# A third seven-product pair in each gate and up group, and low parts by an adding DMA, in a float32 encoder layer

## The chip, the cores and the metric

The kernel runs on one core of a Trainium2 chip. The metric is the device time of one execution in microseconds (us). TensorE is called PE here, VectorE DVE, ScalarE ACT, GpSimd POOL and SyncE SP, as in the profile.

## The reference

One layer of an encoder on 256 tokens of width 2048, all in float32: four mixers side by side, cross attention over 256 memory rows, and a gated feed-forward network, each behind an RMS norm and with a residual; then a last norm. The change is in the feed-forward part:

```python
D_FF = ((8 * D_MODEL // 3 + 255) // 256) * 256        # 5632
def swiglu(h, w_gate_up, w_down):
    gate, up = jnp.split(h @ w_gate_up, 2, axis=-1)
    return (jax.nn.silu(gate) * up) @ w_down
...
    x = x + swiglu(rms_norm(x, norm_g[l, 2]), w_gate_up[l], w_down[l])
return rms_norm(x, final_norm_g)
```

## The kernel before

**Float32 from three matmuls.** A weight W is split into a rounded high part `wh` (ACT copies it to the type that PE multiplies in one pass) and a low part `wl` = W - `wh` (DVE subtracts). Activations are split in the same way. A product is then hi x wh + hi x wl + lo x wh: `part` (L412) issues these three matmuls, 128 x 128 by 128 x 512 each, and all of PE's work in the stage goes through it (L414 to L416).

**The weight stream.** All weights lie in device memory in the order of use, in slabs of 128 x 2048 (1 MB, 16 blocks of 128 columns). `Stream` loads one slab at a time into one of three `raw` buffers (SP issues, L97), and makes halves of 1024 columns: `_half` (L102) with ACT's copy at L124 and DVE's subtraction at L125, into buffers from a pool of three and one extra. `_fill` keeps the half in use and three more made. A raw buffer is free again when the last half of its slab is split.

**Seven products for eight.** A slab of kind N gives four (column block, k) pairs, each with two row halves of the 256 tokens: 4 x 2 x 3 = 24 matmuls. A slab of kind S holds a 2 x 2 arrangement of tiles (two k, two column blocks) and is multiplied by a scheme of seven products instead of eight, 7 x 3 = 21 matmuls. Its sums of weights are made on the fly by `_sums` (L130): four phases (of 1024, 512, 1024 and 1024 columns), four additions on DVE at L137, and a cast (L140) and a subtraction (L141) for each phase. The sums of activations, `z`, are made once by `combine`.

**The gate and up stage.** `gate_up` computes 11 groups of 512 gate and 512 up columns. The first is plain (`gemm_rows`), the other ten go through `paired_rows` with the plan `GROUP` of eight slabs. In a group the gate's two row halves end in PSUM banks `a0` and `a1`, the up's in `b0` and `b1`, and four more banks hold the products `1`, `5`, `6`, `7` that several results share. When the group's last S is done, `mixed` combines these four (ACT's copy at L1034 is its first step), and `gated` adds `a0` and `a1` (L264, `g<-g,pg`) and applies silu (L1044). At the end of the group `upped` adds `b0` and `b1`, multiplies, transposes and stores the result to device memory (`store_turned`, L525). `fetch` brings stored tiles back (L530) and splits them into the `f` tiles of the down product. The next group takes the banks of `a0` and `a1` with its first matmuls.

**Order.** The code issues splits, products and background work (`Background`: `fetch`, `combine` and the like, polled between products) in one program order; a scheduler then fixes the order on each engine before the run. Engines work through their queues in that order, and so does SP with its loads and POOL with its transfers.

**The down stage** (`down`) has 44 k tiles, the `f` list: eight `act` tiles, the `f` tiles, then the tiles that share memory with `z`, then those that share it with `h3`, the input of the gate and up stage. The last two kinds can only be filled when the gate and up stage is over (the second `fetch` of `gate_up`).

Of the kernel before, what the change touches and what calls it, by code (L numbers as in the profile page):

```python
# [13 lines left out]
F32 = mybir.dt.float32  # L14
F32R = mybir.dt.float32r
# [4 lines left out]
ALU = mybir.AluOpType  # L20
# [3 lines left out]
P = 128  # L24
R = 256
D = 2048
KT = D // P
DFF = 5632
FT = DFF // P
# [12 lines left out]
LATE = 12  # L42

GATE_UP = 1920 // 16 + 8
GROUP = "NNSNNSNN"

DOWN = GATE_UP + 80
PASSES = "NNNNNNSNNSNNSNNSNNSNNN", "NNSNSNSNSNSNSNNNNNNNNN"

PAIRED = {a + i for a, plan in [(GATE_UP + 8 * j, GROUP) for j in range(10)] + [(DOWN, PASSES[0]), (DOWN + 22, PASSES[1])]  # L50
          for i, x in enumerate(plan) if x == "S"}

LAG, OWED, SOON, FAR = 1.3, 0.9, 0.01, 18.0
V_NG = 0
# [16 lines left out]
class Stream:  # L71


    def __init__(self, tc, pools, W, bg):
        self.tc, self.nc, self.W, self.bg = tc, tc.nc, W, bg
        self.rawp, self.wp = pools
        self.order = []
        self.n = self.made = 0
        self.after = []
        self.halves = []  # L80
        self.at = self.phase = 0
        self.raw = None
        self.extra = None
        self.places = []

    def _buffers(self, n, m):

        pool = self.extra if self.extra and len(self.halves) % 4 == 3 else self.wp
        at = 48 if any(a <= n < b for a, b in ROWS) else 8
        return (pool.tile([P, 1088], F32R, name=t, tag=t)[:, at:at + m] for t in ("wh", "wl"))  # L90

    def _load(self, n):

        nc = self.nc
        self.raw = self.rawp.tile([P, 2048], F32, name="raw", tag="raw")
        for a, b in zip(CUTS[n], CUTS[n][1:]) if n in CUTS else [(0, 1024), (1024, 2048)] if self.after else [(0, 2048)]:
            (nc.scalar if (n, a) == (0, 0) else nc.sync).dma_start(self.raw[:, a:b], self.W[n // 16][:, a:b])  # L97
            if self.after:
                self.after.pop(0)()

    def _half(self):

        nc, n = self.nc, self.made
        if n % 16 == 0 and self.phase == 0:
            self._load(n)
        if n // 16 in PAIRED:
            return self._sums()
        self.made += 8
        o = (n % 16) * P
        r = self.raw[:, o:o + 1024]  # L110
        if n >= NBLK - HELD:
            parts = []
            for a in (0, 512):
                wh, wl = self.places.pop(0)
                nc.scalar.copy(wh, r[:, a:a + 512])
                nc.vector.tensor_tensor(out=wl, in0=r[:, a:a + 512], in1=wh.bitcast(F32), op=ALU.subtract)
                parts.append((wh, wl))
            self.bg.dve(1024)
            self.halves.append(parts)
            return  # L120
        wh, wl = self._buffers(n, 1024)
        edges = [0, 256, 512, 1024] if n == 0 else [0, 512, 1024] if n == 8 else [0, 1024]
        for a, b in zip(edges, edges[1:]):
            nc.scalar.copy(wh[:, a:b], r[:, a:b])  # L124
            nc.vector.tensor_tensor(out=wl[:, a:b], in0=r[:, a:b], in1=wh[:, a:b].bitcast(F32), op=ALU.subtract)  # L125
        self.bg.dve(1024)
        self.halves.append((wh, wl))
# [108 lines left out]
class Block:  # L236
# [758 lines left out]
    def mlp(self):  # L995
        tc, nc, act = self.tc, self.nc, self.act
        with tc.tile_pool(name="fp", bufs=1) as fp:
            self.gap(fp, 192)
            f = [fp.tile([P, 512], F32R, name=f"f{i}") for i in range(16)]
            z = [fp.tile([P, 1024], F32R, name=f"z{i}") for i in range(2)]  # L1000
            f = act[4:12] + f + [z[i // 2][:, i % 2 * 512:i % 2 * 512 + 512] for i in range(4)] + self.h3
            with tc.tile_pool(name="wy", bufs=1) as self.st.extra:
                self.gap(self.st.extra, 64)
                with tc.tile_pool(name="gp", bufs=2) as gp:
                    self.gate_up(gp, f, z)
# [7 lines left out]
    def gate_up(self, gp, f, z):  # L1013

        nc = self.nc
        box, g, stored = {}, {}, []

        def gate(ps):
            for r in range(2):
                g[r] = gp.tile([P, 512], F32, name=f"g{r}", tag=f"g{r}")  # L1020
                nc.scalar.activation(g[r], ps[r], AF.Silu, scale=box["col"][:, r:r + 1])

        def up(j, ps, h=None):
            h = h or [gp.tile([P, 512], F32, name="h", tag="h") for _ in range(2)]
            for r in range(2):
                u = gp.tile([P, 512], F32, name="u", tag="u")
                self.stt(h[r], ps[r], box["col"][:, r:r + 1], g[r], ALU.mult, ALU.mult)
                self.store_turned(self.ff, 4 * j, r, u, h[r])
            stored.append(self.bg.now)

        def mixed(q1, q5, q6, q7):

            g[0], g[1], h[0], h[1] = (gp.tile([P, 512], F32, name=n, tag=n) for n in ("g0", "g1", "h", "h"))
            nc.scalar.copy(g[0], q1)  # L1034
            self.tt(h[0], g[0], q6, ALU.add)
            self.tt(g[1], h[0], q7, ALU.add)
            self.tt(h[0], q5, h[0], ALU.subtract)
            self.tt(h[1], q5, g[1], ALU.subtract)

        def gated(*ps):  # L1040

            for r in range(2):
                self.tt(g[r], g[r], ps[r], ALU.add)
                nc.scalar.activation(g[r], g[r], AF.Silu, scale=box["col"][:, r:r + 1])  # L1044

        def upped(j, ps):

            for r in range(2):
                self.tt(h[r], h[r], ps[r], ALU.add)
            up(j, h, h)  # L1050

        h = {}

        def fetch(k0, k1, ahead, pause, wait=0):

            m = {}
            for k in range(k0, k1 + ahead):
                if k < k1:
# [22 lines left out]
        arrival = lambda: gp.tile([P, R], F32, name="ar", tag="ar", bufs=4)  # L1081
        last = self.bg.add(self.arrive(self.xf[1], 3, arrival, self.put3, FAR), go=True)
        col = self.bg.add(norm())
        ps = self.gemm_rows("w_gate_up", [0, DFF], self.h3,
                            parts=[(range(8), [0]), (range(8, 12), [0]), (range(12), [1]), (range(12, 16), [0]), (range(12, 16), [1])],
                            before=lambda n: n in (1, 3) and self.bg.drain(self.late if n == 1 else last))
        self.bg.drain(col)
        def combined():
            for ks, z in sums:
                yield from self.combine(z, *(self.h3[k] for k in ks))  # L1090
                yield
        sums = [((2 * i, 2 * i + 1), z[i]) for i in range(GROUP.count("S"))]
        comb = self.bg.add(combined())
        gate(ps[0])
        up(0, ps[1])
        early = self.bg.add(fetch(0, FT - 20, 3, 2.0, 15))
        self.bg.drain(comb)
        for j in range(1, DFF // 512):
            upped(j, self.paired_rows("w_gate_up", [j * 512, DFF + j * 512], self.h3, sums, GROUP, mixed, gated)[0])
        self.bg.drain(early)  # L1100
        self.fetch = self.bg.add(fetch(FT - 20, FT, 6, SOON))

    def down(self, f, sp):

# [751 lines left out]
```

## Time and profile before

| | |
|---|---|
| Time, median of 3 runs | 1443.23 us (1443.13 to 1443.74) |
| The profiled execution: time, span | 1444.41 us, 1442.6 us |
| Granted PE clock | 0.999 |
| Device memory read, written | 298.52 MB, 20.45 MB |
| Raw slab loads of 1024 KB | 246 |

Times in rows are microseconds from the start of the span, durations microseconds unless marked ns. In a timeline row "x3" merges three instructions that follow each other, and what stands in brackets is the idle time ahead of the row and who ended it. In a row of the windows stand, after the window and its length, the busy time and the count of PE, of PE's weight loads, DVE, ACT and POOL, then the granted clock, the DMA engines' mean busy share and GB/s. A row by form has the busy sum, the mean in ns of one, and the idle time ahead with its releasers.

### The profile page before, as it was taken

Reading aid. Unit: us, or ns where it says so; the run is one execution under the profiler, and the core shown is the slowest. Engines: PE = TensorE matmul, PEld = TensorE weight load, DVE = VectorE, ACT = ScalarE, POOL = GpSimd, SP = SyncE. Lnnn points to the kernel's source line nnn. Section 1 sums busy time; section 2 is a strip of 40 time slices with the busy share of each in tenths; the row PEclk is TensorE's granted clock in tenths of the full one; section 3 lists DMA queues with packets and bytes.
Section 4 is the critical chain, followed back from the end, with each engine's and each line's share of the span. In section 5 each row is a group of like instructions: output and inputs, shape, how many; then the busy total and the mean of one; then the engine's idle time right before and its main releaser. Section 6 shows DMA issues by size and latency. Waiting matters only on the chain.

```text
span 1442.6 us, 18337 instructions
## 1 busy us (share of the span) xinstructions
PE 1431.6 (99%) x6631; PEld 1189.5 (82%) x6631; DVE 1121.8 (78%) x1673; ACT 793.9 (55%) x1138; POOL 207.1 (14%) x276
## 2 busy tenths in 40 slices
PE   9999999999999999999999999999999999999997
PEld 7888888888888888888888888888888888788886
DVE  6667868777877667676676888888888888978984
ACT  6566565446655555555554555545555555545553
POOL 0000100013212233530421001111100002000000
PEclk9999999999999999999999999999999999999999
DMA  9886554556667788964785666566566557545553
GB/s 352 288 290 248 204 207 159 176 173 219 202 198 233 235 263 265 274 204 155 238 257 188 233 233 230 198 242 232 200 235 237 211 182 266 204 188 185 223 215 136
DMA packets 60076, 320.19 MB, mean 222 GB/s; under 512 B 9517, under 2 KB 11214, under 8 KB 28368
## 3 DMA queue, kind: packets, MB, share of 16 engines
q1 hardware_dynamic: 46208, 281.11, 54.8%
q0 software_dynamic: 13344, 37.24, 9.6%
q8 instruction: 52, 0.85, 0.2%
q10 hardware_dynamic: 432, 0.66, 0.1%
q14 instruction: 40, 0.33, 0.1%
HBM read 298.52 MB, written 20.45 MB: 221 GB/s over the span
## 4 chain that ended last, share of the span: by engine, by line
PE 98%; DVE 1%; DMA 0%; ACT 0%; issue 0%; SPq 0%; DVEq 0%
PE pg L414 27%; PE pg L416 27%; PE pg L415 27%; PE pg L362 4%; PE pg L363 2%; PE pm L415 2%; PE pm L416 2%; PE pm L414 2%; PE pm L1309 1%; PE pm L988 1%; PE pm L959 1%; DMA raw<-in_W 0%; PE pm L1718 0%; PE pm L960 0%; PE pm L1483 0%
## 5 line engine op out<-in xcount | busy, mean ns | idle before, releaser
L125 DVE TENSOR_TENSOR wl<-raw,wh 128x1024 fp32r<-128x1024 f32 (+1 forms) x441 | 528.0, 1213 | 182.8 <-ACT wh L124 179.4
L124 ACT CAST wh<-raw 128x1024 fp32r<-128x1024 f32 (+1 forms) x441 | 455.3, 1043 | 318.0 <-PE pg L416 252.6
L414 PE MATMUL pg<-wh,act 128*128 128x512 f32 (+1 forms) x1514 | 591.4, 391 | 0.8 <-ACT wh L124 0.8
L415 PE MATMUL pg<-wl,act 128*128 128x512 f32 (+1 forms) x1514 | 589.7, 390 | 1.3 <-DVE wl L125 1.1
L416 PE MATMUL pg<-wh,act 128*128 128x512 f32 (+1 forms) x1514 | 589.5, 389 | 0.0
L414 PEld LDWEIGHTS pg<-wh,act 128*128 128x128 f32 x1514 | 284.6, 188 | 61.2 <-issue 1.5
L415 PEld LDWEIGHTS pg<-wl,act 128*128 128x128 f32 x1514 | 284.5, 188 | 60.7 <-DVE wl L125 2.1
L416 PEld LDWEIGHTS pg<-wh,act 128*128 128x128 f32 x1514 | 284.4, 188 | 59.4 <-DVE act L264 0.2
L140 ACT CAST wh<-raw 128x1024 fp32r<-128x1024 f32 x124 | 116.8, 942 | 194.6 <-PE pg L416 111.9
L141 DVE TENSOR_TENSOR wl<-raw,wh 128x1024 fp32r<-128x1024 f32 x124 | 134.7, 1089 | 65.9 <-ACT wh L140 65.9
L362 PE MATMUL pg<-act,wh 128*128 128x512 f32 x256 | 90.5, 395 | 0.0
L137 DVE TENSOR_TENSOR raw<-raw 128x512 f32<-128x512 f32 x124 | 85.6, 690 | 2.9
L363 PE MATMUL pg<-act,wl 128*128 128x256 f32 x256 | 71.8, 281 | 0.0
L525 POOL DMA_DIRECT2D hidden<-u x22 | 16.6, 760 | 372.3 <-DVE u L523 372.3
L362 PEld LDWEIGHTS pg<-act,wh 128*128 128x128 f32 x256 | 48.1, 188 | 10.4
L363 PEld LDWEIGHTS pg<-act,wl 128*128 128x128 f32 x256 | 48.2, 188 | 0.2
L530 POOL DMA_DIRECT2D tmp<-hidden x44 | 38.8, 887 | 62.4 <-DMA hidden<-u 34.0
L416 PE MATMUL pg<-wh,f 128*128 128x512 f32 x110 | 42.8, 389 | 0.0
L415 PE MATMUL pg<-wl,f 128*128 128x512 f32 x110 | 42.8, 389 | 0.0
L414 PE MATMUL pg<-wh,f 128*128 128x512 f32 x110 | 42.8, 389 | 0.0
L525 POOL DMA_DIRECT2D features<-tmp x32 | 22.7, 715 | 95.7 <-DVE tmp L523 95.7
L530 POOL DMA_DIRECT2D ar<-features x24 | 21.1, 886 | 24.8 <-ACT wh L124 12.4
(358 smaller groups left out, 1469.5 us busy)
## 6 DMA issues: line engine op xcount, KB each, us to landing
raw<-in_W SPq DMA_DIRECT2D x246, 1024.0 KB, 5.0
raw<-in_W SPq DMA_DIRECT2D x11, 512.0 KB, 7.2
hidden<-u POOLq DMA_DIRECT2D x22, 256.0 KB, 3.8
tmp<-hidden POOLq DMA_DIRECT2D x44, 128.0 KB, 3.3
features<-tmp POOLq DMA_DIRECT2D x32, 128.0 KB, 2.7
ar<-features POOLq DMA_DIRECT2D x24, 128.0 KB, 6.2
k<-in_mem SPq DMA_DIRECT2D x8, 256.0 KB, 6.7
keys<-k POOLq DMA_DIRECT2D x8, 256.0 KB, 7.5
```

Of the source, the lines that this page charges most:

```text
L124: nc.scalar.copy(wh[:, a:b], r[:, a:b])
L125: nc.vector.tensor_tensor(out=wl[:, a:b], in0=r[:, a:b], in1=wh[:, a:b].bitcast(F32), op=ALU.subtract)
L137: nc.vector.tensor_tensor(out=s[out], in0=s[a], in1=s[b], op=ALU.add)
L140: nc.scalar.copy(wh, src)
L141: nc.vector.tensor_tensor(out=wl, in0=src, in1=wh.bitcast(F32), op=ALU.subtract)
L362: self.nc.tensor.matmul(p[:, :], wh, slot[:, :], start=start, stop=False)
L363: self.nc.tensor.matmul(p[:, 0:R], wl, slot[:, 0:R], start=False, stop=stop)
L414: self.nc.tensor.matmul(p, hi, wh, start=start, stop=False)
L415: self.nc.tensor.matmul(p, hi, wl, start=False, stop=False)
L416: self.nc.tensor.matmul(p, lo, wh, start=False, stop=stop)
L525: self.nc.gpsimd.dma_start(to[r], u.rearrange("p (k c) -> p k c", c=P))
L530: self.nc.gpsimd.dma_start(t.rearrange("p (g t) -> p g t", t=32), src)
```

## The change

- `GROUP` becomes `NNSNSNSN`: a third S instead of an N. `z` gets a third buffer, `f` gives up two tiles, so 22 instead of 20 of the 44 down tiles are filled after the gate and up stage.
- In the N slabs at places 0, 1, 3 and 5 of a group the second half is made by `_begin`, one slab ahead: ACT copies it to `wh` (rounded), ACT writes the negated rounded weights to `wl`, and a DMA from POOL adds the weights from device memory to `wl`. DVE has no part in it. The two buffers for it are a pool of their own, `lows`. The slab is loaded to its `raw` buffer at that time, one slab earlier in program order than before.
- To make room, `g0` and `g1` have one buffer instead of two, the transposed result goes into `g` instead of a tile `u`, and the last arriving tiles use the space of `h`.
- `combine` runs as background work of the first group instead of behind it, with a pause of 3.0 before each pair.

```diff
-GROUP = "NNSNNSNN"
+GROUP = "NNSNSNSN"
...
+LOW = "LL.L.L.."
+LOWS = {GATE_UP + 8 * j + i for j in range(10) for i, x in enumerate(LOW) if x == "L"}
...
+    def _begin(self, n):
+        nc = self.nc
+        if n not in self.raws:
+            self._load(16 * n)
+        wh, wl = (self.lows.tile([P, 1024], F32R, name=t, tag=t) for t in ("wh", "wl"))
+        src = self.raws[n][:, 1024:2048]
+        nc.scalar.copy(wh, src)
+        nc.scalar.mul(wl, src, -1.0)
+        nc.gpsimd.dma_start(wl, self.W[n][:, 1024:2048], accum_op=ALU.add)
+        self.early[n] = wh, wl
+
     def _half(self):
+        n = self.made // 16
+        begin = self.lows and self.made % 16 == 0 and self.phase == 0 and n + 1 in LOWS
+        self._entry()
+        if begin:
+            self._begin(n + 1)
+
+    def _entry(self):
         nc, n = self.nc, self.made
         if n % 16 == 0 and self.phase == 0:
-            self._load(n)
+            if n // 16 not in self.raws:
+                self._load(n)
+            self.raw = self.raws.pop(n // 16)
         if n // 16 in PAIRED:
             return self._sums()
         self.made += 8
+        if n % 16 and n // 16 in self.early:
+            self.halves.append(self.early.pop(n // 16))
+            return
...
-            f = [fp.tile([P, 512], F32R, name=f"f{i}") for i in range(16)]
-            z = [fp.tile([P, 1024], F32R, name=f"z{i}") for i in range(2)]
+            f = [fp.tile([P, 512], F32R, name=f"f{i}") for i in range(14)]
+            z = [fp.tile([P, 1024], F32R, name=f"z{i}") for i in range(3)]
...
-                u = gp.tile([P, 512], F32, name="u", tag="u")
                 self.stt(h[r], ps[r], box["col"][:, r:r + 1], g[r], ALU.mult, ALU.mult)
-                self.store_turned(self.ff, 4 * j, r, u, h[r])
+                self.store_turned(self.ff, 4 * j, r, g[r], h[r])
...
-        early = self.bg.add(fetch(0, FT - 20, 3, 2.0, 15))
+        early = self.bg.add(fetch(0, FT - 22, 3, 2.0, 15))
         self.bg.drain(comb)
-        for j in range(1, DFF // 512):
-            upped(j, self.paired_rows("w_gate_up", [j * 512, DFF + j * 512], self.h3, sums, GROUP, mixed, gated)[0])
+        with lp as self.st.lows:
+            self.gap(self.st.lows, 96)
+            for j in range(1, DFF // 512):
+                upped(j, self.paired_rows("w_gate_up", [j * 512, DFF + j * 512], self.h3, sums, GROUP, mixed, gated)[0])
+            self.st.lows = None
         self.bg.drain(early)
-        self.fetch = self.bg.add(fetch(FT - 20, FT, 6, SOON))
+        self.fetch = self.bg.add(fetch(FT - 22, FT, 6, SOON))
```

More of the change, by code (lines that the diff above doesn't have):

```diff
@@ L82, in __init__ @@
         self.raw = None
-        self.extra = None
+        self.extra = self.lows = None
         self.places = []
+        self.raws, self.early = {}, {}
     def _buffers(self, n, m):
@@ L94, in _load @@
         nc = self.nc
-        self.raw = self.rawp.tile([P, 2048], F32, name="raw", tag="raw")
+        raw = self.raws[n // 16] = self.rawp.tile([P, 2048], F32, name="raw", tag="raw")
         for a, b in zip(CUTS[n], CUTS[n][1:]) if n in CUTS else [(0, 1024), (1024, 2048)] if self.after else [(0, 2048)]:
-            (nc.scalar if (n, a) == (0, 0) else nc.sync).dma_start(self.raw[:, a:b], self.W[n // 16][:, a:b])
+            (nc.scalar if (n, a) == (0, 0) else nc.sync).dma_start(raw[:, a:b], self.W[n // 16][:, a:b])
             if self.after:
                 self.after.pop(0)()
-    def _half(self):
+    def _begin(self, n):
[8 more added lines that the diff above has]
+        self.early[n] = wh, wl
+    def _half(self):
+        n = self.made // 16
[4 more added lines that the diff above has]
+    def _entry(self):
         nc, n = self.nc, self.made
         if n % 16 == 0 and self.phase == 0:
-            self._load(n)
+            if n // 16 not in self.raws:
+                self._load(n)
+            self.raw = self.raws.pop(n // 16)
         if n // 16 in PAIRED:
@@ L998, in mlp @@
             self.gap(fp, 192)
-            f = [fp.tile([P, 512], F32R, name=f"f{i}") for i in range(16)]
-            z = [fp.tile([P, 1024], F32R, name=f"z{i}") for i in range(2)]
-            f = act[4:12] + f + [z[i // 2][:, i % 2 * 512:i % 2 * 512 + 512] for i in range(4)] + self.h3
+            f = [fp.tile([P, 512], F32R, name=f"f{i}") for i in range(14)]
+            z = [fp.tile([P, 1024], F32R, name=f"z{i}") for i in range(3)]
+            f = act[4:12] + f + [z[i // 2][:, i % 2 * 512:i % 2 * 512 + 512] for i in range(6)] + self.h3
             with tc.tile_pool(name="wy", bufs=1) as self.st.extra:
                 self.gap(self.st.extra, 64)
-                with tc.tile_pool(name="gp", bufs=2) as gp:
-                    self.gate_up(gp, f, z)
+                with tc.tile_pool(name="gp", bufs=1) as gp:
+                    self.gate_up(gp, f, z, tc.tile_pool(name="lp", bufs=2))
                 with tc.tile_pool(name="sp", bufs=1) as sp:
@@ L1011, in mlp, with gate_up @@
                 self.down_end(f, *end)
-    def gate_up(self, gp, f, z):
+    def gate_up(self, gp, f, z, lp):
         nc = self.nc
@@ L1023, in up @@
         def up(j, ps, h=None):
-            h = h or [gp.tile([P, 512], F32, name="h", tag="h") for _ in range(2)]
+            h = h or [gp.tile([P, 512], F32, name="h", tag="h", bufs=2) for _ in range(2)]
             for r in range(2):
-                u = gp.tile([P, 512], F32, name="u", tag="u")
                 self.stt(h[r], ps[r], box["col"][:, r:r + 1], g[r], ALU.mult, ALU.mult)
-                self.store_turned(self.ff, 4 * j, r, u, h[r])
+                self.store_turned(self.ff, 4 * j, r, g[r], h[r])
             stored.append(self.bg.now)
         def mixed(q1, q5, q6, q7):
-            g[0], g[1], h[0], h[1] = (gp.tile([P, 512], F32, name=n, tag=n) for n in ("g0", "g1", "h", "h"))
+            g[0], g[1], h[0], h[1] = (gp.tile([P, 512], F32, name=n, tag=n, bufs=b) for n, b in (("g0", 1), ("g1", 1), ("h", 2), ("h", 2)))
             nc.scalar.copy(g[0], q1)
@@ L1079, in norm, with combined @@
             yield
-        arrival = lambda: gp.tile([P, R], F32, name="ar", tag="ar", bufs=4)
+        spare = [gp.tile([P, 512], F32, name="h", tag="h", bufs=2) for _ in range(2)]
+        spare = iter([x[:, i:i + R] for x in spare for i in (0, R)])
+        arrival = lambda: next(spare)
         last = self.bg.add(self.arrive(self.xf[1], 3, arrival, self.put3, FAR), go=True)
         col = self.bg.add(norm())
+        def combined():
+            for ks, z in sums:
+                yield 3.0
+                yield from self.combine(z, *(self.h3[k] for k in ks))
+        sums = [((2 * i, 2 * i + 1), z[i]) for i in range(GROUP.count("S"))]
+        comb = self.bg.add(combined())
         ps = self.gemm_rows("w_gate_up", [0, DFF], self.h3,
@@ L1087, in gate_up @@
         self.bg.drain(col)
[L1088 to L1093, printed above, removed]
         gate(ps[0])
         up(0, ps[1])
-        early = self.bg.add(fetch(0, FT - 20, 3, 2.0, 15))
+        early = self.bg.add(fetch(0, FT - 22, 3, 2.0, 15))
         self.bg.drain(comb)
-        for j in range(1, DFF // 512):
-            upped(j, self.paired_rows("w_gate_up", [j * 512, DFF + j * 512], self.h3, sums, GROUP, mixed, gated)[0])
+        with lp as self.st.lows:
[3 more added lines that the diff above has]
+            self.st.lows = None
         self.bg.drain(early)
-        self.fetch = self.bg.add(fetch(FT - 20, FT, 6, SOON))
+        self.fetch = self.bg.add(fetch(FT - 22, FT, 6, SOON))
     def down(self, f, sp):
```

## The prediction

> **What bounds the kernel now.** I read the page's busy table and chain first, then the stage of the change product by product, then the queues inside one product.
>
> ```profile
> PE 1431.6 (99%) x6631; PEld 1189.5 (82%) x6631; DVE 1121.8 (78%) x1673; ACT 793.9 (55%) x1138; POOL 207.1 (14%) x276
> PE 98%; DVE 1%; DMA 0%; ACT 0%; issue 0%; SPq 0%; DVEq 0%
> ```
>
> TensorE (PE) is busy for 99% of the span and makes up 98% of the chain that ended last. A saved matmul can therefore be a saved pitch of PE, provided the others keep up. The line that copies `q1` in `mixed` runs once per gate and up group, so it is the clock of the stage. The windows cut the stage at that line.
>
> ```profile
> L1034 ACT COPY g<-pm x10: 579/579/580, 806.7 to 1186.1; 128x512 f32<-128x512 f32 x10
> ```
>
> ```profile
> 806.71:848.87 42.16, 42.16 (x188) 34.93 (x187) 36.27 (x44) 22.93 (x29) 5.03 (x6) 1.00 0.63 225
> 1059.65:1101.80 42.15, 42.15 (x188) 34.92 (x187) 36.01 (x44) 21.69 (x25) 5.04 (x6) 1.00 0.62 225
> ```
>
> Nine periods take 379.4 us, 42.16 each. By the plan a group has 2 S slabs of 7 products x 3 matmuls and 6 N slabs of 24, so 186 matmuls: 42.16 / 186 = 0.2267 us a matmul. (The windows count 188, because the modelled ends overlap the cut.) PE is busy for the whole of each window, so no group loses anything now. One S slab lasts 21 x 0.2267 = 4.76 us, one N slab 5.44, one N half 2.72.
>
> **Matmuls removed.** A third S in place of an N takes out 3 of 186 matmuls: 0.68 us a group, 10 groups, **6.80 us**. That is all that the change can gain. The other parts decide how much of it stays.
>
> **VectorE (DVE), the amount.** Rows of the stage by form, and one run of splits:
>
> ```profile
> L137 DVE TENSOR_TENSOR raw<-raw 128x512 f32<-128x512 f32 x80 | 55.2, 690 | 1.9
> L141 DVE TENSOR_TENSOR wl<-raw,wh 128x512 fp32r<-128x512 f32 x20 | 13.7, 686 | 0.0
> ```
>
> ```profile
> 1084.88 0.61 DVE L264 TENSOR_TENSOR tmp<-tmp 128x128 f32<-128x128 f32 x2
> 1086.29 1.23 DVE L141 TENSOR_TENSOR wl<-raw,wh 128x1024 fp32r<-128x1024 f32 x1 [0.79 <-ACT wh L140]
> 1087.64 4.63 DVE L125 TENSOR_TENSOR wl<-raw,wh 128x1024 fp32r<-128x1024 f32 x4
> ```
>
> A split in a run costs 4.63 / 4 = 1.16 us. An S slab costs four additions at 0.69, three full splits and a half one at 0.69: 6.93. It replaces an N slab's two splits (2.32), and four low parts leave DVE (4.64). The difference is 6.93 - 2.32 - 4.64 = -0.03 us a group: DVE still works 36 us, now in 41.48 instead of 42.16, 87% against 85%. By amount it is no bound. Between two S slabs there is now one N slab instead of two, but its second half is a low one: 6.93 + 1.16 = 8.1 us of DVE in 4.76 + 5.44 = 10.2 us of PE. That fits as well.
>
> **DVE, the order at the end of a group.** The third S stands at place 6 of 8, the second stood at place 5. So `mixed` and `gated` have one N slab (5.44 us) before the next group needs the banks of `a0` and `a1`, where they had two (10.88). PE, then DVE, after an S slab at place 5:
>
> ```profile
> 1058.44 0.39 PE L414 MATMUL pm<-wh,act 128*128 128x512 f32 x1
> ```
>
> ```profile
> 1059.77 1.23 DVE L141 TENSOR_TENSOR wl<-raw,wh 128x1024 fp32r<-128x1024 f32 x1 [0.69 <-ACT wh L140]
> 1061.19 3.50 DVE L125 TENSOR_TENSOR wl<-raw,wh 128x1024 fp32r<-128x1024 f32 x3 [0.20 <-ACT wh L124]
> 1064.61 0.68 DVE L264 TENSOR_TENSOR h<-g,pm 128x512 f32<-128x512 f32 x1
> 1065.21 1.22 DVE L125 TENSOR_TENSOR wl<-raw,wh 128x1024 fp32r<-128x1024 f32 x1
> 1066.34 0.68 DVE L264 TENSOR_TENSOR g<-h,pm 128x512 f32<-128x512 f32 x1
> 1066.94 0.68 DVE L264 TENSOR_TENSOR g<-g,pg 128x512 f32<-128x512 f32 x1
> 1067.54 0.68 DVE L264 TENSOR_TENSOR h<-pm,h 128x512 f32<-128x512 f32 x1
> 1068.14 0.68 DVE L264 TENSOR_TENSOR h<-pm,g 128x512 f32<-128x512 f32 x1
> 1068.74 1.21 DVE L125 TENSOR_TENSOR wl<-raw,wh 128x1024 fp32r<-128x1024 f32 x1
> 1069.87 0.68 DVE L264 TENSOR_TENSOR g<-g,pg 128x512 f32<-128x512 f32 x1
> 1070.47 1.22 DVE L125 TENSOR_TENSOR wl<-raw,wh 128x1024 fp32r<-128x1024 f32 x1
> 1073.83 1.27 DVE L264 TENSOR_TENSOR h<-h,pg 128x512 f32<-128x512 f32 x2
> 1075.02 1.41 DVE L268 SCALAR_TENSOR_TENSOR h<-h,rc,g 128x512 f32<-128x512 f32 x2
> 1076.35 1.30 DVE L523 STREAM_TRANSPOSE u<-h 128x512 f32<-128x512 f32 x2
> ```
>
> The S slab starts at 1058.44. The two `g<-g,pg` rows are what frees the banks: `a0` at 1067.62 (+9.18), `a1` at 1070.55 (+12.11). Before, the next group wanted them at 4.76 + 10.88 = +15.64 and, its second row half three matmuls later, +16.32. Afterwards it wants them at +10.20 and +10.88. With today's order and pace `a0` has 1.0 us left and `a1` is 1.2 us late. Two things pull it in. Five splits stand ahead of the second `g<-g,pg`; with the new plan one of the next five halves is a low one, so one split (1.16) falls away. And a low half holds none of the four split buffers, so the last splits of the S slab, which today wait for PE to give one back, may start up to half an N half earlier. What is left is between 0 and 1.2 us a group; I take 0.05, so **+0.5 us** over ten groups, with 0 and 12 as the ends. `upped` (about 3.7 us, from 1073.83) then starts behind it and ends some 15 us after the S began, long before the first S of the next group at place 2 wants DVE.
>
> **The adding DMA.** No row shows an addition in a transfer. What can be read is how long it may take. The tightest is slab 5. Its raw load reuses the buffer of slab 2, an S, whose last split ends some 2.56 us after it began (1059.77 + 1.23 - 1058.44 in the S above). Then the load, two ACT passes, the issue:
>
> ```profile
> raw<-in_W SPq DMA_DIRECT2D x246, 1024.0 KB, 5.0
> ...
> hidden<-u POOLq DMA_DIRECT2D x22, 256.0 KB, 3.8
> ```
>
> ```profile
> L124 ACT CAST wh<-raw 128x1024 fp32r<-128x1024 f32 x118 | 121.4, 1050 | 53.8 <-PE pg L416 47.9 <-PE pm L416 5.9
> ...
> L530 POOL DMA_DIRECT2D tmp<-hidden x32 | 28.2, 888 | 38.9 <-DMA hidden<-u 34.0 <-ACT wh L140 4.9
> ```
>
> 2.56 + 5.0 + 2 x 1.05 + 0.89 = 10.6 us; PE wants the low part at 4.76 + 5.44 + 4.76 + 2.72 + 0.23 = 17.9. So 7.3 us are allowed; for slab 1 the same sum over S, N, N and an N half gives 8.0, slabs 0 and 3 have no less. The 512 KB are bounded below by 3.8 (256 KB, plain) and above by 10 (twice the 5.0 of 1024 KB). I take 6, between the rows and nearest to the 1024 KB one with some sharing, so **0 us**; at the upper end 2.7 us are missed in slab 5, 2.0 in slab 1. The cover is the low pool's second buffer and the start one slab ahead. GpSimd (POOL) issues in order: four times 0.89 is added to its 5.0 us a group, but the L530 row sat 34.0 us behind landings of `hidden<-u`, and an adding DMA queued there waits too.
>
> ```profile
> 1083.79 3.52 POOL L530 DMA_DIRECT2D tmp<-hidden x4 [4.93 <-ACT wh L140]
> ```
>
> With a group's start at 1058.44 + 15.64 = 1074.08 these stand 9.7 to 13.2 us into it, in places 1 and 2, ahead of slab 3's adding DMA, which is wanted only about 10 us later.
>
> Load: queue by queue in one group,
>
> ```profile
> q1 hardware_dynamic: 1152, 8.39, 53.3%
> q0 software_dynamic: 352, 1.05, 8.8%
> ```
>
> four halves add 2.1 MB: at q1's rate 13%, at q0's 18%, so the DMA share goes from 0.62 to about 0.78. The Trainium skill (Collectives: The Full Stack, the section on the bandwidth ceiling and why AG, RS and AR differ) says that a reduction in the DMA engines is slow because each add reads two sources, and measures it at half the rate of a copy. By that rule the 13% become 27% and the share 0.89, an estimate; no run here shows it yet, and the sum above does not use it.
>
> **ScalarE (ACT).** 3.6 casts for the S, less 2, plus 4 negations at 1.05: about 6 us more on 22 of 41.48. It is idle enough. What matters is that a copy waiting for a raw load holds the queue: between 0 and the 2 us of one such stall. The order on a queue goes by what is ready rather than by the program: the `q1` copy runs ahead of three casts that the code issues before it,
>
> ```profile
> 1059.64 0.58 ACT L1034 COPY g<-pm 128x512 f32<-128x512 f32 x1
> 1060.11 2.98 ACT L124 CAST wh<-raw 128x1024 fp32r<-128x1024 f32 x3
> ```
>
> so I take 0.
>
> **The passage into `down`.** Two more of the 44 `f` tiles are filled late (22 instead of 20), where DVE is already the chain:
>
> ```profile
> 1223.94 1.35 issue
> ...
> 1238.79 1.15 DVE wl L125
> ...
> 1239.98 0.50 PE pg L415
> ```
>
> ```profile
> PE pg L415 <- DVE wl L125: 0.6, 1, 0.6
> PE pg L415 <- DVE wl L141: 0.2, 1, 0.2
> ```
>
> PE loses 0.8 us here today. Two splits of a 256-wide tile at half the 0.69 row add 0.7, and `upped` of the last group ends up to 1.3 us later against PE. So 0 to 2.0 more; I take **+1.0**. The combinations moved into the first product have a cover: DVE is idle for over half of it.
>
> ```profile
> 765.00:775.00 10.00, 10.00 (x46) 8.29 (x45) 4.02 (x5) 5.10 (x6) 0.00 (x0) 1.00 0.60 210
> ```
>
> Single `g` and the transpose into `g` cost nothing: the store lands in 3.8 us, the next write to `g` comes some 25 us after it.
>
> **Sum.** -6.80 + 0.5 + 0 + 1.0 = -5.3 us against the profiled execution's 1444.41 (span 1442.6): 1439.1. The median of the three runs, 1443.23, is 1.2 below that execution, so **1438.0**. About 0.2% (2.9 us) is what a measurement can tell from no change.
>
> **Rivals.**
> *The banks come late.* DVE's order at the end of a group stays as it is, or an ACT negation slips in ahead of the casts, and `a1` is late by 1.2 to 2 us each time: +12 to +20, so -6.8 + 1 + 12 = about 1449, and up to 1457. It decides from 0.6 us a group on. For it: the static order above; against it: the split that falls away. Chance 0.17, a third of it with so little delay that the result is within 0.2%.
> *The adding DMA lands late.* From 7.3 us on, each microsecond costs 10 us for slab 5, from 8.0 on another 10 for slab 1. At 10 us: 27 + 20, less the gain, about 1484; at 8 us, 1445. For it: no row shows such a transfer, and the rule of two reads (Trainium skill, above) points to the 1024 KB row or worse. Chance 0.16.
> *The stage was not PE's after all*, the slots are filled by waits, and nothing changes: against it stand the full PE windows. Chance 0.05.
> Forecast, 1436.4 (nothing lost) to 1440.3: 0.62.
>
> **Range and chances.** 1436.3 to 1449: that leaves out the upper end of both slow rivals, about 0.17, and very little below. Faster 0.62, same 0.11 (a third of the banks' case, and the last rival), slower 0.27. The forecast's own range is 1436.4 to 1440.3.
>
> **What would show it.** Right: the period of the `q1` copy at 41.48, PE full in each window, DVE near 36 us a group, landing of the adding DMA under 7 us. Wrong: PE waiting for a `g<-g,pg` at a group's first matmul (banks), for a low tile from a DMA at the second half of slabs 5 or 1 (late landing), or over 2.8 us of PE waits between the last group and the first S of `down`.

## The result: slower, by what fills the low halves

The changed kernel takes 1464.22 us (median of 4 runs, 1461.92 to 1466.33) against 1443.49 for the kernel before in the same runs: a ratio of 1.0141, interval 1.0128 to 1.0154. The forecast was 1438.0 with a range up to 1449.0; size and sign are wrong. The profiled execution took 1463.94 us, its span is 1461.8. Line numbers below are those of each kernel's own code; in the kernel after, the matmuls are L443 to L445, a plain half's cast and split L153 and L154, those of a sum L169 and L170, the low half's copy, negation and adding DMA L112 to L114, the bank additions L293 and the `q1` copy L1062.

The busy table and the chain that ended last, of after:

```profile
PE 1437.1 (98%) x6601; PEld 1184.4 (81%) x6601; DVE 1125.1 (77%) x1703; ACT 839.7 (57%) x1198; POOL 242.4 (17%) x314
PE 19%; DVE 2%; DMA 1%; ACT 0%; issue 0%; ACTq 0%; DVEq 0%
```

The chain could be followed back to about 1130 us only and says nothing of most groups. PE runs 30 matmuls fewer and yet is busy for 5.5 us more, at a granted clock of 0.995 instead of 0.999: a first sign that some of them ran more slowly. The windows over nine periods of the `q1` copy (window and length, then busy time and count of PE, weight loads, DVE, ACT and POOL, granted clock, DMA share, GB/s), before and then after:

```profile
806.70:1186.10 379.40, 379.40 (x1676) 314.33 (x1675) 323.41 (x387) 202.32 (x231) 38.26 (x46) 1.00 0.62 222
```

```profile
817.70:1207.70 390.00, 379.25 (x1630) 305.45 (x1628) 320.16 (x400) 238.17 (x279) 69.42 (x80) 0.99 0.86 261
```

A period is 43.33 us (390.0 / 9) instead of 42.16, where 41.48 was forecast. PE was full before and now is idle for 10.75 us. DVE's work hardly changed. ACT's rose by 35.9 us, the DMA share from 0.62 to 0.86. PE's waits of after, from 760 to 1300 us:

```profile
PE pg L444 <- DVE wl L154: 5.3, 5, 2.2
PE pm L443 <- ACT wh L169: 2.9, 2, 2.5
PE pg L444 <- DMA wl<-in_W: 2.4, 4, 1.0
PE pm L444 <- DVE wl L170: 2.0, 3, 0.8
PE pg L443 <- DVE g L293: 0.5, 2, 0.3
PE pg L443 <- ACT wh L153: 0.3, 1, 0.3
```

Three kinds stand here: ordinary splits that come late (L153, L154, L169, L170), the adding DMA, and the bank additions. (The longest wait of the first row, 2.2 us, stands in the passage into `down`, in the later tables too.) The view leaves out short idles and the slow matmuls behind a stall. So I also added up, between 760 and 1290 us, by how much each matmul's start lay beyond 0.2267 us after the one before, and put each piece down to the last wait named ahead of it. After loses 26.3 us: late splits 14.6, the adding DMA 4.3, banks 3.0, the passage into `down` 4.4. Before loses 1.6, all in the passage. 26.3 - 1.6 - 6.8 saved = 17.9 of the 19.2 us between the spans. The figures below called "lost" are from this sum.

**How an ordinary split comes late.** The timelines of ACT, DVE and PE of after, at one place:

```profile
900.21 1.05 ACT L112 CAST wh<-raw 128x1024 fp32r<-128x1024 f32 x1 [1.57 <-DMA raw<-in_W]
901.16 1.05 ACT L113 ACTIVATE wl<-raw 128x1024 fp32r<-128x1024 f32 x1
902.12 2.92 ACT L153 CAST wh<-raw 128x1024 fp32r<-128x1024 f32 x3
```

```profile
903.18 3.50 DVE L154 TENSOR_TENSOR wl<-raw,wh 128x1024 fp32r<-128x1024 f32 x3 [3.10 <-ACT wh L153]
```

```profile
904.47 0.50 PE L444 MATMUL pg<-wl,act 128*128 128x512 f32 x1 [0.76 <-DVE wl L154]
```

ACT first waits for a raw load, then makes the two passes for the next slab's low half, and only then the cast of a half that is wanted at once. DVE sat idle for 3.10 us until this cast, PE until DVE's split. The two passes take 1.91 us of ACT's queue and PE waited for 0.76: without them the cast would have been in time, by about 1 us. Without the hold of 1.57 us ahead of them it would have been, too. ACT is busy for only 61% of the nine periods, but its order is fixed.

The dearest case is the hold in front of slab 5's passes:

```profile
976.41 1.05 ACT L112 CAST wh<-raw 128x1024 fp32r<-128x1024 f32 x1 [6.02 <-DMA raw<-in_W]
977.36 1.05 ACT L113 ACTIVATE wl<-raw 128x1024 fp32r<-128x1024 f32 x1
978.32 1.98 ACT L169 CAST wh<-raw 128x1024 fp32r<-128x1024 f32 x2
```

```profile
979.40 0.80 PE L443 MATMUL pm<-wh,z 128*128 128x512 f32 x1 [2.49 <-ACT wh L169]
980.66 0.80 PE L444 MATMUL pm<-wl,z 128*128 128x512 f32 x1 [0.47 <-DVE wl L170]
981.25 0.63 PE L445 MATMUL pm<-wh,z 128*128 128x512 f32 x1
981.68 0.63 PE L443 MATMUL pm<-wh,z 128*128 128x512 f32 x1
...
985.52 0.49 PE L443 MATMUL pg<-wh,act 128*128 128x512 f32 x1
```

Slab 4, an S, waits here for its cast behind a copy that waits for slab 5. Then something unexpected: from 981.25 to 985.52 the matmuls follow each other at 0.427 us instead of 0.2267, and the granted clock is 0.50 from 978.90 to 985.73 (last section). These rows lose about 6.2 us, of which the two idles are 3.0.

**How the transfers come late.** Queues and issues over the same nine periods, of after and then of before (issues: count, size, median us from issue to landing):

```profile
q1 hardware_dynamic: 10224, 74.45, 52.2%
q0 software_dynamic: 7898, 27.05, 33.9%
...
raw<-in_W SPq DMA_DIRECT2D x71, 1024.0 KB, 7.0
wl<-in_W POOLq DMA_DIRECT2D x35, 512.0 KB, 6.6
```

```profile
q0 software_dynamic: 2784, 8.39, 7.7%
...
raw<-in_W SPq DMA_DIRECT2D x72, 1024.0 KB, 5.0
```

The 35 adding transfers are 18.35 MB. POOL's queue rose from 7.7% of 379.4 us (29.2) to 33.9% of 390.0 (132.2); with 8.70 MB of other traffic at before's rate (30.3), they took 101.9 us, 5.55 us a MB. The raw loads take 52.2% of 390.0 / 74.45 = 2.73 us a MB. If the other traffic did go at before's rate, an adding byte costs twice a byte of the raw loads. The raw loads themselves land in 7.0 us instead of 5.0.

### The profile page after: what moved, and what is told of

The parts are those of the page before. It is cut to its first block, busy times and chain, and to the rows that moved or that the text cites. A ratio compares the mean times of both kernels' runs of the same rounds, so it can differ in the third digit from the quotient of the medians.

```text
span 1461.8 us, 18396 instructions
## 1 busy us (share of the span) xinstructions
PE 1437.1 (98%) x6601; PEld 1184.4 (81%) x6601; DVE 1125.1 (77%) x1703; ACT 839.7 (57%) x1198; POOL 242.4 (17%) x314
## 5 line engine op out<-in xcount | busy, mean ns | idle before, releaser
L154 DVE TENSOR_TENSOR wl<-raw,wh 128x1024 fp32r<-128x1024 f32 (+1 forms) x383 | 460.1, 1212 | 206.4 <-ACT wh L153 204.3
L443 PE MATMUL pg<-wh,act 128*128 128x512 f32 (+1 forms) x1454 | 570.2, 392 | 2.7 <-ACT wh L153 1.7
L445 PE MATMUL pg<-wh,act 128*128 128x512 f32 (+1 forms) x1454 | 566.4, 390 | 0.0
L153 ACT CAST wh<-raw 128x1024 fp32r<-128x1024 f32 (+1 forms) x383 | 394.7, 1041 | 284.0 <-PE pg L445 228.4
L443 PEld LDWEIGHTS pg<-wh,act 128*128 128x128 f32 x1454 | 273.9, 188 | 65.9 <-DVE g L293 4.3
L445 PEld LDWEIGHTS pg<-wh,act 128*128 128x128 f32 x1454 | 273.5, 188 | 57.1 <-DVE act L293 0.2
L169 ACT CAST wh<-raw 128x1024 fp32r<-128x1024 f32 (+1 forms) x164 | 150.9, 940 | 147.8 <-DVE raw L166 70.0
L170 DVE TENSOR_TENSOR wl<-raw,wh 128x1024 fp32r<-128x1024 f32 (+1 forms) x164 | 173.8, 1086 | 55.6 <-ACT wh L169 55.6
L166 DVE TENSOR_TENSOR raw<-raw 128x512 f32<-128x512 f32 x164 | 113.1, 690 | 4.0
L114 POOL DMA_DIRECT2D wl<-in_W x38 | 34.0, 894 | 255.6 <-ACT wl L113 241.7
L112 ACT CAST wh<-raw 128x1024 fp32r<-128x1024 f32 x38 | 39.7, 1045 | 37.6 <-DMA raw<-in_W 37.6
L113 ACT ACTIVATE wl<-raw 128x1024 fp32r<-128x1024 f32 x38 | 40.2, 1057 | 21.3 <-DMA raw<-in_W 17.4
L443 PE MATMUL pm<-wh,z 128*128 128x512 f32 x90 | 36.1, 401 | 2.9 <-ACT wh L169 2.9
L444 PE MATMUL pm<-wl,z 128*128 128x512 f32 x90 | 36.1, 401 | 2.0 <-DVE wl L170 2.0
```

The source lines that it names most:

```text
L112: nc.scalar.copy(wh, src)
L113: nc.scalar.mul(wl, src, -1.0)
L166: nc.vector.tensor_tensor(out=s[out], in0=s[a], in1=s[b], op=ALU.add)
L169: nc.scalar.copy(wh, src)
L170: nc.vector.tensor_tensor(out=wl, in0=src, in1=wh.bitcast(F32), op=ALU.subtract)
L443: self.nc.tensor.matmul(p, hi, wh, start=start, stop=False)
```

## The experiments

The theory after the result: the low halves' own work is the cause, ACT's passes by their place in the order and the adding DMA by its traffic. The rivals: the third S with its late banks is the cause; the passes' wait for the early raw load is it, not the passes; or only the addition in the transfer is.

**The two halves of the change.** First the third S without low parts:

```diff
-LOW = "LL.L.L.."
+LOW = "........"
```

> Third S kept, no low part by DMA (LOW empty, all splits on DVE again). Theory 1, ACT held: the loss comes from ACT's early copy waiting in its queue for a raw load, so that the splits behind it are late; without early copies ACT's waits for raw loads go, DVE has 40.6 us of work in 41.48, and the time is 1440 to 1447. Theory 2, traffic: the loss comes from the adding DMA's doubled reads, which make raw loads late; same as theory 1 here. Theory 3, DVE: the third S asks more of DVE than fits around it, banks and splits are late; then this is the worst kernel, 1465 or more.

Measured: 1456.75 us, ratio 1.0087 [1.0070, 1.0104]. The window of its nine periods:

```profile
810.50:1184.00 373.50, 373.50 (x1649) 308.75 (x1648) 353.47 (x415) 207.54 (x228) 21.51 (x27) 1.00 0.61 219
```

A period is 41.50 us and PE full. DVE works 39.3 us in each, 95%, and nothing waits for it. So the third S alone gives the ten groups their full gain, without any relief of DVE. The loss is elsewhere: 22.4 us in the passage. POOL's timeline and PE's waits there:

```profile
1198.30 1.49 POOL L554 DMA_DIRECT2D hidden<-g  x2 [40.00 <-DVE g L552]
1199.79 10.53 POOL L559 DMA_DIRECT2D tmp<-hidden  x12
```

```profile
PE pg L445 <- DVE f L293: 5.0, 1, 5.0
PE pg L445 <- DVE act L293: 3.8, 1, 3.8
```

The early `fetch` is background work that is polled only while the planner reckons DVE to be less than 0.9 us behind (`OWED`). With 39 us of DVE in each group that is seldom so: between 916 and 1199 us of this trace not one tile was fetched. The fetches ran all together when the groups were over, against a PE that already wanted the tiles. The low parts thus do have a use, but it lies in the planner's budget and not in the stage.

Then the low parts in the old plan, and two of the four in the new one:

```diff
-GROUP = "NNSNSNSN"
+GROUP = "NNSNNSNN"
-LOW = "LL.L.L.."
+LOW = "LL.LL..."
```

> Two S per group as before, low parts of four halves by the adding DMA (slabs 0, 1, 3, 4). Theories 1 and 2: early copies and doubled reads are still there, slower than before: 1447 to 1460. Theory 3: DVE has 4.6 us a group less to do than before, so nothing is late: 1442 to 1445.

```diff
-LOW = "LL.L.L.."
+LOW = "L..L...."
```

> Third S, low parts only in slabs 0 and 3, whose raw buffers do not come from an S slab. Theory 1: the early copies of slabs 1 and 5, which wait for a load that starts when an S is split, are gone; most of the loss goes: 1443 to 1450. Theory 2: half the added traffic, so about half the loss: 1452 to 1457. Theory 3: DVE has 2.3 us a group more to do: 1465 or more.

The first took 1489.48 us, 1.0320 [1.0305, 1.0336]. Its PE waits and its landing:

```profile
PE pg L444 <- DMA wl<-in_W: 26.4, 12, 3.4
```

```profile
wl<-in_W POOLq DMA_DIRECT2D x38, 512.0 KB, 9.7
```

With an unchanged number of matmuls the low parts cost 46 us: the rival of the late adding DMA in full. They land at a median of 9.7 us here and of 6.4 in after. The twelve late ones are six each of slabs 3 and 4, of which POOL issues the second 3.2 us behind the first in five of six cases: slab 3's land after 9.2 to 10.7 us, slab 4's after 11.7 to 16.0. In after no two are issued closer than 5.2 us. The second took 1460.98, 1.0118 [1.0103, 1.0133], and lost 9.2 us to the DMA and 9.0 to late splits. Half the low halves bring back 3 of the 21 us; the loss does not go by their number.

**The parts of a low half.** Four kernels take it apart. Without the addition (a plain transfer of the same bytes):

```diff
-        nc.gpsimd.dma_start(wl, self.W[n][:, 1024:2048], accum_op=ALU.add)
+        nc.gpsimd.dma_start(wl, self.W[n][:, 1024:2048])
```

> As the change, but the DMA copies the weights instead of adding them (the subtraction of the low parts is left out), so it reads one source. Theory 2: its time in the DMA queues halves (share about 0.87 to 0.75 in the stage), landings and raw loads come earlier, and the loss falls to less than half: 1444 to 1453. Theory 1: the raw load of the early copy still starts only when its buffer comes free, ACT still waits: 1456 to 1464. Theory 3: unchanged, 1462 to 1466.

Without ACT's passes, with two plain transfers that together read as many bytes as the adding one, but write twice as many:

```diff
-        nc.scalar.copy(wh, src)
-        nc.scalar.mul(wl, src, -1.0)
-        nc.gpsimd.dma_start(wl, self.W[n][:, 1024:2048], accum_op=ALU.add)
+        nc.gpsimd.dma_start(wh, self.W[n][:, 1024:2048])
+        nc.gpsimd.dma_start(wl, self.W[n][:, 1024:2048])
```

> As the change, but ACT makes neither the copy nor the negation: the two tiles of a low half are filled by two plain DMAs from POOL (both then hold the whole weights), so the bytes read equal those of the adding DMA, and ACT has 4 x 2.1 us a group less. Theory 4, ACT's added passes: they stand in ACT's order ahead of casts that have about 1 us to spare, whether or not they wait for a load; then late splits shrink from 14.6 us to under 4 and the time is 1446 to 1453. Theory 2, the traffic: raw loads still land after 8 to 11 us in the bunch, late splits stay above 9 us: 1456 to 1465.

With the passes and no transfer:

```diff
-        nc.gpsimd.dma_start(wl, self.W[n][:, 1024:2048], accum_op=ALU.add)
```

> As the change, but without the adding DMA (the low tile holds the negated high part only); ACT's copy and negation, their order and the early loads stay. Theory 4: late splits stay near 13 us, no wait for an adding DMA: 1456 to 1461. Theory 2: raw loads land in 5 us again, late splits go: 1443 to 1450.

With neither, the early raw load kept:

```diff
-        nc.scalar.copy(wh, src)
-        nc.scalar.mul(wl, src, -1.0)
-        nc.gpsimd.dma_start(wl, self.W[n][:, 1024:2048], accum_op=ALU.add)
-        self.early[n] = wh, wl
+        self.early[n] = self.kept
```

> As the change, with the slab loaded early in program order as there, but the four low halves are two constant tiles: neither ACT's passes nor the adding DMA (these halves of the weights are left out of the product). With passes and adding DMA 1464.2, without the passes 1453.5, without the DMA 1451.1. If these two are all that costs in the groups, the groups stay at 41.5 us and only the passage is left (2.8 us more than before): -6.8 + 2.8, so 1439 to 1442. If the early loads, or the order at the group's end (banks), cost something by themselves, the groups are at 42 or more and the time is 1444 to 1450.

| low half by | us | ratio | lost in the groups |
|---|---|---|---|
| passes and adding DMA (after) | 1464.22 | 1.0141 [1.0128, 1.0154] | 21.9: splits 14.6, DMA 4.3, banks 3.0 |
| passes and plain DMA | 1456.44 | 1.0092 [1.0077, 1.0107] | 16.5: splits 13.8, banks 2.7 |
| passes alone | 1451.10 | 1.0047 [1.0033, 1.0062] | 12.2: splits 9.9, banks 2.3 |
| the traffic alone | 1453.49 | 1.0069 [1.0055, 1.0082] | 15.1: banks |
| neither | 1440.35 | 0.9973 [0.9963, 0.9982] | 0.2 |

The window of the last one's nine periods:

```profile
811.30:1185.00 373.70, 373.70 (x1649) 309.05 (x1648) 322.49 (x402) 177.17 (x211) 37.40 (x45) 1.00 0.64 225
```

41.52 us a period, PE full: with neither passes nor traffic the forecast's saving is there whole, banks included, and 0.9973 is near the forecast's 0.9963 (1438.0 / 1443.23). From 1440.35 the passes, with their wait for the early load, cost 10.8 us; the adding transfer costs 13.1 more behind them (1464.22 - 1451.10), 23.9 in all. The traffic alone also costs 13.1, but its two plain transfers weigh more than the adding one: POOL's queue takes 40.4% of 388.7 us there (157.0, against 132.2), at a DMA share of 0.90. That the two single costs add up to the whole is in part luck, and the runs of one kernel spread over 2 to 5 us.

Nor is only the addition to blame. A plain transfer behind the passes costs 5.3 us (1456.44 - 1451.10), the addition 7.8 more. In the plain kernel POOL's queue takes 23.0% of 386.4 us (88.9) for 27.14 MB; less 30.6 for 8.79 MB of other traffic that is 3.18 us a MB, so an adding byte costs 1.75 times a plain one of the same queue. The raw loads land in 7.0 us with either.

In PE's waits of the kernel with the passes alone the ordinary splits lead again:

```profile
PE pg L443 <- DVE wl L153: 4.7, 5, 2.2
PE pm L442 <- ACT wh L168: 1.4, 2, 1.1
```

With the traffic alone it is another wait that grows. PE's waits of that kernel, then ACT, DVE and PE at the start of one group:

```profile
PE pg L442 <- DVE g L292: 9.8, 9, 3.5
PE pg L443 <- DVE wl L153: 2.2, 1, 2.2
```

```profile
862.37 1.05 ACT L152 CAST wh<-raw 128x1024 fp32r<-128x1024 f32 x1 [4.67 <-DMA raw<-in_W]
```

```profile
863.45 1.23 DVE L153 TENSOR_TENSOR wl<-raw,wh 128x1024 fp32r<-128x1024 f32 x1 [1.05 <-ACT wh L152]
864.59 0.68 DVE L292 TENSOR_TENSOR g<-g,pg 128x512 f32<-128x512 f32 x1
```

```profile
865.33 0.50 PE L442 MATMUL pg<-wh,act 128*128 128x512 f32 x1 [0.79 <-DVE g L292]
```

A raw load lands late, its cast waits, its split stands in DVE's order ahead of the second `g<-g,pg`, and PE waits for the bank. The split itself was in no hurry. Each kernel's order is planned anew, so the same late load shows up under other names.

**Is it the wait for the early load?** The passes read the current slab's raw buffer, which has to be there anyway:

```diff
-        src = self.raws[n][:, 1024:2048]
+        src = self.raw[:, 1024:2048]
```

> As the change, but the early copy and negation read the slab that is already there instead of the next one (the low halves then hold the wrong weights); loads, DMAs, ACT and POOL work stay. Theory 1, ACT held by the raw load: the late splits (14.6 us of PE's lost time in the trace of the change) go, the adding DMAs start earlier, 1444 to 1452. Theory 2, the DMA's traffic and lateness: ACT's wait only moves to the splits themselves, 1458 to 1465.

The two tiles of a low half still add up to the weights here, since `wl` takes away what `wh` holds. 1460.37 us, 1.0118 [1.0102, 1.0133]; splits still lose 13.4 us, banks 5.1, the DMA nothing. PE's waits, and ACT's waits for raw loads from 780 to 1210 us, of after and then of this kernel:

```profile
PE pg L444 <- DVE wl L154: 6.8, 9, 2.2
PE pg L443 <- DVE g L293: 2.8, 3, 1.3
PE pm L444 <- DVE wl L170: 2.4, 4, 0.8
...
PE pm L443 <- ACT wh L169: 0.4, 1, 0.4
```

```profile
ACT wh L112 <- DMA raw<-in_W: 37.6, 22, 6.0
...
ACT wh L169 <- DMA raw<-in_W: 17.5, 9, 2.5
ACT wl L113 <- DMA raw<-in_W: 17.4, 7, 4.7
```

```profile
ACT wh L169 <- DMA raw<-in_W: 32.4, 15, 5.2
ACT wh L153 <- DMA raw<-in_W: 20.7, 9, 4.4
ACT wh L112 <- DMA raw<-in_W: 20.3, 11, 3.1
```

The single long hold in front of an S is gone (PE's wait for L169: 2.9 in after, 0.4 now), and the rest stayed. Of the passes' own waits (L112 and L113), 55.0 us in after, 20.3 are left, for the current slab isn't always there in time either; the ordinary casts' waits for raw loads rose from 17.5 to 53.1. As the cause of the whole this rival falls: with more than half of the passes' wait gone, about 4 of the 24 us came back. But the wait was not taken out in full, and in the kernel with the passes alone L112 still waits for 33.4 us. How its 10.8 us divide between the passes and their waits is not shown.

The other remedy, to begin a low half only behind the last split of the previous slab:

```diff
-        begin = self.lows and self.made % 16 == 0 and self.phase == 0 and n + 1 in LOWS
+        begin = self.lows and (self.phase == 3 if n in PAIRED else self.made % 16 == 8) and n + 1 in LOWS
```

> As the change, but a low half is begun behind the last split of the slab ahead of it instead of behind the first: the load has half a slab to three quarters of a slab more before ACT's copy asks for it, the adding DMA that much less before PE asks for its result. Theory 1: late splits shrink from 14.6 us to under 5. But an adding DMA that lands after 6 to 10 us has then only 4 to 7: PE waits for it 20 us or more in place of 4, so 1465 to 1490. If neither, 1450 to 1460.

1467.84 us, 1.0159 [1.0145, 1.0173]: splits 13.4, the DMA 6.2, banks 3.0. A later start moves a little from the splits to the adding DMA. Neither of the two places tried in ACT's order has room for both.

**Can the third S pay without low parts?** The poll limit of the first experiment was raised to 4.0 in the ten groups, then lifted:

```diff
-            if self.owed < OWED and self.now >= e[1]:
+            if self.owed < self.limit and self.now >= e[1]:
...
+        self.bg.limit = 4.0
```

> The third S alone, no low part by DMA, and the limit of modelled DVE work above which background steps are held back is raised from 0.9 to 4.0 us during the ten groups, so that the early fetch is done there and not all at once behind them. If the loss of the run with the third S alone (1456.8) lies only in the fetch that was put off, the groups stay at 41.5 us (DVE 39.3 + 0.8 for two to three fetched tiles a group) and the passage loses 2 to 5 us: 1438 to 1443. If DVE has no room for the fetch beside three S, the groups grow past 42.2: 1445 or more.

```diff
-        self.bg.limit = 4.0
+        self.bg.limit = 1e9
```

> The third S alone with the fetch never held back by modelled DVE work in the ten groups (the limit of 4.0 was passed again from the sixth group on: 11 tiles were still split in one run behind the last group). If DVE has the 0.8 us a group to spare that 39.3 of 41.48 leaves, the groups stay at 41.5 and the passage loses 3 to 5 us as in the change: 1438 to 1442, faster than both. If the split tiles push group ends late, 1443 to 1450.

1452.71 us, 1.0061 [1.0048, 1.0073], and 1446.75, 1.0020 [1.0011, 1.0029]. At 4.0 the limit was passed again from the sixth group on, and the passage lost 16.4 us; without a limit 8.4, with the period still at 41.73. The account of the first experiment stands: the held-back fetches are most of its loss. To let DVE catch up in the passage, each S of the first down product was put one place later:

```diff
-PASSES = "NNNNNNSNNSNNSNNSNNSNNN", "NNSNSNSNSNSNSNNNNNNNNN"
+PASSES = "NNNNNNNSNNSNNSNNSNNSNN", "NNSNSNSNSNSNSNNNNNNNNN"
```

> As the run before, and the S slabs of the first pass of the down stage one place later, so that DVE has one N slab (5.44 us of PE) more for the late fetch and the combinations before the first S. If the passage is short of DVE time alone, its loss falls by 2 to 4 us: 1435.5 to 1439. If it is the loads' landing, no gain over the run before.

1444.70 us, 1.0007 [0.9998, 1.0016]: no difference from before, with 6.2 us still lost in the passage. Last, the lifted limit was kept up to the first S of `down`:

> As the run before, and the background steps stay unheld until the first S of the down stage, too. In the run before, DVE sat idle for 0.8 to 1.5 us in each of eight N halves between 1205 and 1226 us while late tiles were still to be fetched, and PE then lost 6.2 us in the passage. If those 7 us are used, the passage loses 1 to 3 us, the gain of the third S shows, and the time is 1438.5 to 1441.5. If the fetch is limited by its transfers (loads that land after 3 to 6 us), no gain: 1443 to 1446.

1448.69 us, 1.0032 [1.0020, 1.0044]. A miss: the passage lost about 11.7 us, 4.5 of them in one wait for a cast whose tile had not landed.

```profile
PE pg L444 <- ACT act L302: 4.5, 1, 4.5
```

No full version was found that beats the kernel before. Several expectations were missed: the first three kernels, the two with the passes or the traffic alone and this last one lie outside every range that was given for them, the one with the traffic by 0.5 us.

## Why the prediction was wrong

- **The matmuls, -6.80: right.** Two kernels run the ten groups at 41.50 and 41.52 us; 41.48 was forecast.
- **DVE by amount, -0.03 a group: near enough.** 320.16 / 9 = 35.6 us against 35.9. The step did not see that the stage would have taken 39.3 as well, so that the groups did not need the relief whose price they paid.
- **ScalarE, "I take 0": the first step that failed.** ACT's work rose by 4.0 us a group where 6 was reckoned, and yet the passes with their waits cost 10.8 us in all. The bound of "the 2 us of one such stall" was too low twice over: the hold was up to 6.02 us, and hold and passes come again with each of 38 low halves, ahead of casts with about 1 us to spare at the place shown. Which of the two does more stays open. The argument that the order goes by what is ready leaned on one early `q1` copy. The order is fixed before the run.
- **The adding DMA, 0: the second.** The tightest place was named wrongly. All five late arrivals are slab 1's, issued just behind the `q1` copy, where the raw loads bunch; these land in 9.5 to 11.9 us, others in 5.5 to 8.9. The 6 us taken for a landing were near the median (6.4) and too low for slab 1, in part past the bound of 10; but there were about 10.8 us from issue to use at the worst of them, so this wait itself costs only 4.3. What the step left out is what the traffic does to others: raw loads at 7.0 us instead of 5.0, and the splits or banks behind them. With its own wait the transfer costs 13.1 us, the difference between the kernels with and without it. The sum was made from the one transfer's deadline and not from everybody's.
- **The DMA share, "about 0.78": wrong, and the rule beside it right.** By the Trainium skill (Collectives: The Full Stack, the section on the bandwidth ceiling and why AG, RS and AR differ) each add reads two sources and goes at half the rate. The measured 5.55 against 2.73 us a MB agrees; against the 3.18 of a plain transfer in the same queue it is 1.75 times. The 0.89 of the prediction was read from a window of 42.15 us; over the real 43.33 it becomes 0.87, and 0.86 was measured. The plain transfers gave 0.77, as the 0.78 said.
- **The banks, +0.5: too small, 3.0.** The second `g<-g,pg` of a group comes 0.2 to 0.5 us late in most groups, as the static order said. With neither passes nor traffic it is never late: the term grew from late loads and casts, not from the third S.
- **The passage, +1.0 with an end of 2.0: 2.8 more than before (4.4 against 1.6).** The place and the sign were right. With neither passes nor traffic it is 3.2 more (4.8 against 1.6).
- **Of the rivals,** the adding DMA's named the right engine and landings of 8 to 10 us, but not the way: the waits it priced cost 4.3 us, its traffic behind other names the rest. An ACT pass ahead of the casts stood only in the banks' rival, priced by the bank; no rival had the passes as a cost of their own. The corrected sum is -6.8 + 3.2 + 10.8 + 13.1 = +20.3, against 20.7 measured. Its last two terms are differences between these kernels, so the agreement is bookkeeping and not a further proof.

## What to carry to other kernels

Before paying to relieve an engine, show that something waits for it in the stage in question: here 39 us of DVE in 41.5 cost nothing in the groups, and the relief cost 24. An engine at 60% that works in a fixed order isn't free; price a new pass by the slack of the instruction right behind it, times the number of passes. Price an added transfer by what it does to the landings of all the others, count an adding one about twice (1.75 to 2 here), and ask which background work a planner will hold back once an engine looks full.

## What the runs showed of the hardware

PE runs at half its clock behind some short idles, and the granted clock shows it. In after it is 0.50 from 978.90 to 985.73 us, around the end of the idle of 2.49 us at 979.40, and from 1258.79 to 1262.21, behind an idle of 2.23 us that ended at 1257.59; the matmuls there follow each other at 0.427 us instead of 0.2267. Of the 26.3 us lost in after about 4 are this slower pitch, of the 46 us of the low parts in the old plan, with nine such stretches, about 14.

The stretches are 6.83 and 3.41 us long in after, one to three times 3.41 in all the runs (those at the end of the program aside), and within a run they start whole multiples of 3.41 us apart: 40.96, 47.79 and 10.24 us between the first four of the low parts in the old plan. The length of an idle alone does not decide. The same wait of 2.24 us in the passage had no such stretch behind it in the kernels with the plain transfer and with the later start (granted clock 1.00). It may depend on where the idle falls between two multiples; no run here tested that.

The Trainium skill (TensorE: Matmul & The Clock Gate, Part 1) says that the clock is halved after an idle window of about 3.4 us and gives 426.7 ns as the pitch of a 512-column matmul then. The trace agrees with the pitch; the idles that brought it on here were shorter than this window.
